# The order of every engine's instructions, taken from the scheduler's other machine model

## The chip, the cores and the metric

The kernel runs on one core of a Trainium2 chip. The time is the device time of one execution in microseconds. The profile names the engines PE (TensorE matmul), PEld (its weight loads), DVE (VectorE), ACT (ScalarE), POOL (GpSimd) and SP (SyncE, which here only issues DMAs).

## The reference, cut to what matters

One layer of a diffusion backbone over 1024 latent tokens with 1024 features and a context of 256 tokens, all in float32. Three sub-layers follow each other; each norms, modulates and gates its own result:

```python
h_lat = half_ffn(h_lat, ..., w13_a, w2_a)      # h + 0.5*gate*norm(swiglu(modulate(norm(h))))
h_ctx = half_ffn(h_ctx, ..., w13_a, w2_a)
h_lat, _ = token_mixing(h_lat, h_ctx, ...)     # one projection w_in of IN_WIDTH columns, then
#   a 2-D Fourier transform of 512 channels, and a bidirectional chunked mLSTM of 4 heads
#   (conv + silu on q and k, gates, chunks of 128 tokens, the context's final states first),
#   merged with sigmoid gates through w_four, w_mproj and w_out
h_lat = half_ffn(h_lat, ..., w13_b, w2_b)

def swiglu(u, w13, w2):
    a, b = jnp.split(u @ w13, 2, axis=-1)      # 1024 x 5632, then 2816 x 1024
    return (jax.nn.silu(a) * b) @ w2
```

## The kernel before, in words

Every large product is a sum of three matmuls on parts of the operands (`mm3`, L151 to L153): both operands are split into a high and a low part, and the product of the two low parts is left out. Tokens stand in two blocks of 512. A matmul is 128 x 128 against 128 x 512 and takes one bank of the accumulation memory.

Weights come in units of 1024 columns. `wload` issues the load on SP's queue (L124), `wunit` makes the high part on ACT (L138) and the low part on DVE (L139). The rings for the raw unit, the high part and the low part (`wr`, `wh`, `wl`) have three buffers each. Other tiles stand in rings with a fixed number of buffers too (`SLOTS`), and the accumulators in three: four banks `mm` for the large products, two `aux` and two `qc` for small ones.

The stages, in the order of time in the profile: setup and the first modulation; the first feed-forward half of the latents (`ffn_in`, a product of 2 x 2 blocks in seven multiplications, then `proj_out`); the same for the context; the token mixing (from about 930 to 2040 us), in which the projections of q, k, v and of the gates run among the small steps of the mLSTM and of the Fourier transform; the second feed-forward half, whose last product is token-major (`final`) and goes to the output.

The small steps are generators. `later` puts them in a list with a rate, and `tick`, called between the matmuls of a large product, advances them by that rate times the part of a weight unit done; `defer` calls a function a given number of units later. So the text of the program already has the small steps woven between the large products. Small matmuls that the prediction speaks of: L996 (transposing the gate rows, `gate_rows`), L1013 (the chunk's contribution to the state, `state_step`), L1039 and L1051 (the context's keys, `key_in` and `key_out`), L1198 (query times state), L1221 (`turn`), L1228 (`values`), L1239 (`store`), L1333 and L1341 (`fourier_rest`). Stores that it names: L474 (the gated product, `glu`) and L1112 (`gate_proj`).

The text is not the order in which the engines run. The tile framework records all instructions with their dependences. When the context closes, its scheduler plays the program through on a model of the machine. An engine of the model that is free takes, of its instructions whose operands and buffers are ready, the one written earliest. The order in which the model starts them becomes the fixed list of each engine and of each issuing queue, the buffers that tiles get are given out in the same play-through, and semaphores are put where one list needs another's result. On the chip each engine works its list from front to back. There are two such models in the framework: the default one and a second, the "timeline" model. They differ in what they charge for an instruction, a transfer and the way between engines.

Of the kernel before, what the change touches and what calls it, by code (L numbers as in the profile page):

```python
# [34 lines left out]
class Kernel:  # L35
# [15 lines left out]
    def defer(self, fn, parts=1.0):  # L51
        """fn is issued that many units of weights later, when its operands are sure to be there"""
        self.deferred.append([parts, fn])
# [92 lines left out]
    def mm3(self, out, st, mv, first, last):  # L146
        """out += st^T mv over the three products of the parts that carry weight in float32."""
        sh, sl = st
        mh, ml = mv
        mul = self.nc.tensor.matmul  # L150
        mul(out, sh, mh, start=first, stop=False)  # L151
        mul(out, sh, ml, start=False, stop=False)  # L152
        mul(out, sl, mh, start=False, stop=last)  # L153

# [66 lines left out]
    def ada_first(self):  # L221
        """shift and scale of the first half-step for both streams, the first half of the features"""
        nc = self.nc
        w = self.a["w_ada"][0]
        for ch in (1, 0):
# [5 lines left out]
            row = self.s512("t")  # L231
# [34 lines left out]
    def ada_cols(self, row, streams, ch, hf):  # L266
        """rows of the two streams -> columns, with the bias"""
# [9 lines left out]
    def pre(self, s, i, halves=(0, 1)):  # L277
        """per-feature scale g_pre*(1+scale) of sub-layer i (0..2) and the shift"""
# [12 lines left out]
    def post(self, s, i):  # L291
        """per-feature gate*g_post of sub-layer i, with the half of the half-steps"""
# [8 lines left out]
    def rstd_of(self, ssq, n, width, name=None):  # L301
        """(ssq/width + eps)^-0.5 on [128, n]"""
# [7 lines left out]
    def rows_bcast(self, rstd, n):  # L310
        """[128 tokens, n] -> PSUM [128, n*128], the value of each token in every partition"""
# [6 lines left out]
    def spread(self, rstd, T):  # L318
        """rstd in every partition"""
# [7 lines left out]
    def sumsq(self, tiles, T, out, name=None):  # L327
        """feature-major tiles [128, T] -> out[0]: rstd [128 tokens, T/128]"""
# [18 lines left out]
    def load_x(self, src, T, name, out, keep=False, tag="o"):  # L347
        """tokens from DRAM: the transpose to scratch, rstd of each token; out: scratch, rstd, tiles"""
# [44 lines left out]
    def prenorm(self, tiles, rstd, T, s, i, u, ds=range(ND)):  # L393
        """u = norm(h)*g*(1+scale) + shift, split; tiles: callable d -> [128, T]; rstd: list of one"""
# [26 lines left out]
    # The first product takes both blocks of 512 tokens at once, each pair of feature tiles as a product  # L421
    # of 2x2 blocks (token block x half of the inputs, half of the inputs x feature tile) in seven multiplications
    # after Winograd:
    #   s1 = a21+a22  s2 = s1-a11  s3 = a11-a21  s4 = a12-s2
    #   t3 = b22-b12  t2 = t3+b11  t1 = b12-b11  t4 = b21-t2
    #   p1 = a11 b11  p2 = a12 b21  p3 = s4 b22  p4 = a22 t4  p5 = s1 t1  p6 = s2 t2  p7 = s3 t3
    #   c11 = p1+p2  c12 = p1+p6+p5+p3  c21 = p1+p6+p7+p4  c22 = p1+p6+p7+p5
    NP = NF // 2

    def operands(self, tiles, rstd, u, s, i, out):  # L430
        """the sums over the normed tokens of both blocks, split; u: those of the first block"""
# [38 lines left out]
    def glu(self, p, g, gate, gs, j, b):  # L470
        """j: which feature tile of the pair, b: block of tokens"""
# [4 lines left out]
    def pair_weights(self, w, q, n0, W, p1s):  # L476
        """the combinations of weights of one pair of feature tiles (q even: those under silu, q odd: the others),
        in stages"""
# [50 lines left out]
    def pair_products(self, q, n0, W, U, gs, gates):  # L529
        """the products of one pair of feature tiles; yields the number of each"""  # L530
# [49 lines left out]
    def half_unit(self, w, p, k0):  # L580
        """half of the inputs of the first feature tiles of pair p"""
        return [w[:, k0 : k0 + 4, c : c + P] for c in (2 * p * P, FF + 2 * p * P)]

    def ffn_in(self, w13, n0, first, U, gs, early=0, mid=None):
        """silu(u w1)*(u w3) of both blocks to scratch; the products of the first block come first for n0 pairs.
        early: for so many pairs those of the first half of the inputs come before mid is called.
        Yields when room for operands of the next product comes free."""
# [77 lines left out]
    def g_loader(self, gs, b):  # L665
        """two feature tiles of the gated product, split"""
# [11 lines left out]
    def proj_out(self, w2, g, load=None, then=None, g2=None):  # L678
        """[K, 1024] weights on a feature-major operand: eight [128, 512] results.
        load: makes the operand during the first pass over it; then: the next operand, g2, during the last"""  # L680
# [29 lines left out]
    def residual(self, o, T, s, i, base, scr=None, c0=0, r=None, name=None):  # L710
        """in place: base + gate*norm(o); to scratch, with its rstd in r"""
        nc = self.nc
        q = []
# [96 lines left out]
    def ctx_residual(self, os, ssq, base, scr, r):  # L810
        """[two token tiles x two halves] -> h1 feature-major [128, 256] tiles to scratch"""
# [26 lines left out]
    def conv(self, xs, T, ct, out):  # L838
        """silu of the depthwise convolution over tokens (k scaled by 1/16); xs has a column to either side"""
# [10 lines left out]
    def tok_major(self, wcol, stat, ntt, sinks):  # L850
        """512 columns of w_in from wcol for ntt token tiles, token-major; sinks(tt, psum)"""
# [17 lines left out]
    def v_sink(self, v, nchunk, base, brow):  # L869
        """v: per head of the pair a list of tiles [128, 2, 257], two chunks each, a column of ones behind"""  # L870
# [27 lines left out]
    def gate_rows(self, psums, T, m0, full, nm, out):  # L898
        """rows 0-3: forward heads, rows 32-35: backward heads; T tokens per psum.
# [811 lines left out]
```

## Time and profile before

| | |
|---|---|
| median of 3 runs | 2786.73 us (2786.63 to 2790.77) |
| span of the profiled execution | 2784.4 us |
| PE busy | 2710.0 us (97%), 11937 matmuls |
| PEld busy | 2155.0 us (77%) |
| DVE busy | 1781.4 us (64%), 3147 instructions |
| ACT busy | 1071.4 us (38%), 1758 instructions |
| POOL busy | 97.7 us (4%), 214 instructions |
| granted TensorE clock, mean | 0.995 |
| DMA | 439.98 MB, mean 158 GB/s |

The span runs from the first to the last instruction of the profiled execution; the time of that execution is not listed beside it, and the median of the runs stands 2.3 us above the span. The matmuls are pipelined and the ends in their records are modelled, so an interval in which PE counts as busy may still hold less work than another. Idle time of an engine counts only where the engine sets the end.

### The profile page before, as it was taken

Reading aid. Unit: us, or ns where it says so; the run is one execution under the profiler, and the core shown is the slowest. Engines: PE = TensorE matmul, PEld = TensorE weight load, DVE = VectorE, ACT = ScalarE, POOL = GpSimd, SP = SyncE. Lnnn points to the kernel's source line nnn. Section 1 sums busy time; section 2 is a strip of 40 time slices with the busy share of each in tenths; the row PEclk is TensorE's granted clock in tenths of the full one; section 3 lists DMA queues with packets and bytes.
Section 4 is the critical chain, followed back from the end, with each engine's and each line's share of the span. In section 5 each row is a group of like instructions: output and inputs, shape, how many; then the busy total and the mean of one; then the engine's idle time right before and its main releaser. Section 6 shows DMA issues by size and latency. Waiting matters only on the chain.

```text
span 2784.4 us, 33892 instructions
## 1 busy us (share of the span) xinstructions
PE 2710.0 (97%) x11937; PEld 2155.0 (77%) x11937; DVE 1781.4 (64%) x3147; ACT 1071.4 (38%) x1758; POOL 97.7 (4%) x214
## 2 busy tenths in 40 slices
PE   8899999999999999999999999999999999999998
PEld 5688887778787777777777777778887788887777
DVE  6787777676585439465463765555759777763455
ACT  4543233343364336233332333334345323243443
POOL 1100000000000001000000000000002000000000
PEclk9999999999999999999999999999999999999999
DMA  8763434666486545324233442356547443335574
GB/s 302 242 204 110 137 110 147 205 227 203 142 259 204 171 133 173 90 79 143 71 97 104 140 135 58 108 163 208 190 149 233 136 136 114 118 106 164 196 249 166
DMA packets 414936, 439.98 MB, mean 158 GB/s; under 512 B 22105, under 2 KB 290946, under 8 KB 414768
## 3 DMA queue, kind: packets, MB, share of 16 engines
q1 hardware_dynamic: 413376, 436.01, 49.4%
q0 software_dynamic: 1248, 1.75, 0.3%
q8 instruction: 94, 1.54, 0.2%
q14 instruction: 74, 0.61, 0.1%
q10 hardware_dynamic: 144, 0.07, 0.0%
HBM read 360.10 MB, written 77.64 MB: 157 GB/s over the span
## 4 chain that ended last, share of the span: by engine, by line
PE 76%; DMA 9%; DVE 8%; issue 5%; ACT 2%; SPq 0%; POOL 0%; DVEq 0%; POOLq 0%; ACTq 0%
PE mm L153 22%; PE mm L151 22%; PE mm L152 22%; PE aux L1013 2%; DMA m<-r_l 2%; DVE wl L139 1%; PE qc L1198 1%; DMA ld<-in_w_ada_dram 1%; DMA wr<-gs 1%; DMA wr<-in_w_a_dram 1%; DMA wr<-in_w_b_dram 1%; DVE g L144 1%; DMA ld<-h 1%; ACT wh L138 1%; PE mm L230 1%
## 5 line engine op out<-in xcount | busy, mean ns | idle before, releaser
L139 DVE TENSOR_TENSOR wl<-wr,wh 128x1024 fp32r<-128x1024 f32 x342 | 414.1, 1211 | 376.6 <-ACT wh L138 375.6
L151 PE MATMUL mm<-g,wh 128*128 128x512 f32 (+1 forms) x1400 | 574.3, 410 | 5.5 <-ACT wh L138 5.5
L138 ACT CAST wh<-wr 128x1024 fp32r<-128x1024 f32 x342 | 352.9, 1032 | 558.5 <-PE mm L152 269.4
L153 PE MATMUL mm<-g,wl 128*128 128x512 f32 (+1 forms) x1400 | 558.8, 400 | 0.6 <-DVE wl L139 0.5
L152 PE MATMUL mm<-g,wh 128*128 128x512 f32 (+1 forms) x1400 | 558.4, 399 | 0.1
L151 PEld LDWEIGHTS mm<-g,wh 128*128 128x128 f32 (+1 forms) x1400 | 264.3, 189 | 67.1 <-ACT wh L138 6.6
L153 PEld LDWEIGHTS mm<-g,wl 128*128 128x128 f32 (+1 forms) x1400 | 263.7, 188 | 63.1 <-DVE wl L139 2.7
L152 PEld LDWEIGHTS mm<-g,wh 128*128 128x128 f32 (+1 forms) x1400 | 264.0, 189 | 58.7 <-issue 0.7
L151 PE MATMUL mm<-g,o 128*128 128x512 f32 x704 | 278.0, 395 | 0.0
L152 PE MATMUL mm<-g,o 128*128 128x512 f32 x704 | 277.9, 395 | 0.0
L153 PE MATMUL mm<-g,o 128*128 128x512 f32 x704 | 277.2, 394 | 0.0
L550 DVE TENSOR_TENSOR t<-mm,t 128x512 f32<-128x512 f32 x228 | 153.2, 688 | 85.5 <-PE mm L153 83.7
L151 PE MATMUL mm<-u,wh 128*128 128x512 f32 (+1 forms) x424 | 168.3, 399 | 8.1 <-DVE m L649 4.9
L153 PE MATMUL mm<-u,wl 128*128 128x512 f32 (+1 forms) x424 | 166.7, 396 | 3.1 <-DVE wl L139 3.1
L152 PE MATMUL mm<-u,wh 128*128 128x512 f32 (+1 forms) x424 | 167.7, 395 | 0.1
L153 PEld LDWEIGHTS mm<-g,o 128*128 128x128 f32 x704 | 132.3, 188 | 31.5
L151 PEld LDWEIGHTS mm<-g,o 128*128 128x128 f32 x704 | 132.2, 188 | 31.3
L152 PEld LDWEIGHTS mm<-g,o 128*128 128x128 f32 x704 | 132.2, 188 | 30.8
L151 PE MATMUL mm<-wh,g 128*128 128x512 f32 x280 | 112.2, 405 | 1.6 <-ACT b L1111 1.6
L152 PE MATMUL mm<-wl,g 128*128 128x512 f32 x280 | 111.4, 398 | 1.7 <-DVE wl L139 1.7
L153 PE MATMUL mm<-wh,g 128*128 128x512 f32 x280 | 111.1, 397 | 0.0
L151 PE MATMUL mm<-wh,u 128*128 128x512 f32 x272 | 108.9, 401 | 0.0
(545 smaller groups left out, 4199.7 us busy)
## 6 DMA issues: line engine op xcount, KB each, us to landing
wr<-in_w_a_dram SPq DMA_DIRECT2D x134, 512.0 KB, 4.1
wr<-in_w_b_dram SPq DMA_DIRECT2D x104, 512.0 KB, 3.9
wr<-in_w_in_dram SPq DMA_DIRECT2D x80, 512.0 KB, 3.5
gs<-m SPq DMA_DIRECT2D x88, 256.0 KB, 2.9
wr<-gs SPq DMA_DIRECT2D x44, 512.0 KB, 4.2
ld<-in_w_ada_dram SPq DMA_DIRECT2D x64, 256.0 KB, 2.8
ld<-h SPq DMA_DIRECT2D x56, 256.0 KB, 3.7
wr<-in_w_a_dram SPq DMA_DIRECT2D x40, 256.0 KB, 4.1
```

The costliest lines, as they stand in the source:

```text
L138: nc.scalar.copy(hv, rv)
L139: nc.vector.tensor_tensor(lv, rv, hv.bitcast(F32), op=ALU.subtract)
L144: self.nc.vector.tensor_tensor(lo, src, hi.bitcast(F32), op=ALU.subtract)
L151: mul(out, sh, mh, start=first, stop=False)
L152: mul(out, sh, ml, start=False, stop=False)
L153: mul(out, sl, mh, start=False, stop=last)
L230: nc.tensor.matmul(pt[:2, :], self.sc[:, k, :], t, start=k == 0, stop=k == ND - 1)
L550: add = lambda o, x, y: nc.vector.tensor_tensor(o, x, y, op=ALU.add)
L1013: nc.tensor.matmul(pt[:, :257], kw[:, i * P : (i + 1) * P], vaug, start=True, stop=True)
L1198: nc.tensor.matmul(pt[:, :257], at(q, i, c), C[:, i * 257 : (i + 1) * 257], start=i == 0, stop=i == 1)
```

## The change

One argument is added where the context is opened. It makes the scheduler play the program through on the timeline model in place of the default one. Instructions, tiles, rings and written order stay as they are. The other hunks of the diff delete comments and docstrings and leave the line numbers as they were; one of them stands here for all.

```diff
@@ -85,7 +85,7 @@
         self.bg.extend(gens)
         self.rate = rate
 
-    # ---- tiles ----
+
     def name(self, s):
         self.n += 1
         return f"{s}_{self.n}"
...
@@ -1704,7 +1704,7 @@
         arrays[f"in_{n}_dram"] = x
         a[n] = nc.dram_tensor(f"in_{n}_dram", x.shape, mybir.dt.from_np(x.dtype), kind="ExternalInput").ap()
     out = nc.dram_tensor("out_0_dram", (1, SEQ, D), F32, kind="ExternalOutput").ap()
-    with tile.TileContext(nc) as tc:
+    with tile.TileContext(nc, schedule_with_timeline_sim=True) as tc:
         emit(tc, a, out)
     r = _run(nc, [arrays], core_ids=[0])
     return r.results[0]["out_0_dram"]
```

## The prediction

> **What bounds the kernel now.** I read the page first (busy shares and clock), then the busy time by stretch, then PE's own waits in the stage that loses most, then a few microseconds of the timeline there.
>
> ```profile
> span 2784.4 us, 33892 instructions
> PE 2710.0 (97%) x11937; PEld 2155.0 (77%) x11937; DVE 1781.4 (64%) x3147; ACT 1071.4 (38%) x1758; POOL 97.7 (4%) x214
> PE 76%; DMA 9%; DVE 8%; issue 5%; ACT 2%; SPq 0%; POOL 0%; DVEq 0%; POOLq 0%; ACTq 0%
> ```
>
> PE is the bound: 97% busy, and 76% of the chain that ended last. Its work does not change here, so only the 74.4 us in which it idles (2784.4 - 2710.0) can be won, and any new idle time on it is lost in full. The same in stretches (the columns are start:end, length, then busy us and instruction count for PE, PEld, DVE, ACT, POOL, then the granted clock and the DMA share and GB/s):
>
> ```profile
> 0.00:130.00 130.00, 115.03 (x489) 81.64 (x489) 81.95 (x134) 66.78 (x126) 18.03 (x34) 0.99 0.85 282
> 130.00:470.00 340.00, 337.96 (x1452) 273.67 (x1453) 266.64 (x408) 114.26 (x188) 4.56 (x4) 0.99 0.45 136
> 1000.00:1900.00 900.00, 869.75 (x3907) 688.10 (x3906) 522.44 (x1349) 330.65 (x646) 39.85 (x144) 0.99 0.39 118
> 2170.00:2495.00 325.00, 325.00 (x1401) 262.76 (x1400) 240.86 (x372) 100.25 (x162) 0.00 (x0) 1.00 0.38 117
> 2495.00:2784.40 289.40, 271.69 (x1202) 217.17 (x1200) 139.03 (x166) 112.25 (x151) 4.43 (x5) 0.99 0.58 196
> ```
>
> The first row is the start, where data must first arrive: PE idles 15.0 us. The second and fourth are the two long products of the feed-forward halves: 2.0 us idle of 665, with DVE at 78% and 74%. The third is the token mixing: 30.2 us idle of 900. The last is the final product and the store: 17.7 us, part of it the end itself, where nothing is left for PE.
>
> **What the change moves.** No instruction is added or removed; the other hunks of the diff delete comments. What is rewritten is the order in which each of the five queues (PE, DVE, ACT, POOL, SP) holds its instructions, and with it which buffer of a ring a tile gets and so whose release it waits for. Each queue runs its list in order, so a wait on one instruction holds everything behind it (the row at 1047.72 below is one). The order comes from a play-through: an engine that is free takes the earliest written instruction that is ready by the model. Where the model is early about a result, the chip waits at that place; where it is late, ready work stands too far back. I cannot see from the trace what the second model charges, so I price the places at which the order decides.
>
> Term 1, the small matmuls in the token mixing. These (transposes, states, products of the recurrence) are written between the projections' matmuls and go into PE's list wherever the model thought their operands there. PE's waits from 1000 to 1900 us (us in all, times, longest):
>
> ```profile
> PE aux L1221 <- DVE m L1212: 6.2, 5, 2.4
> PE aux L1013 <- DVE m L1192: 6.2, 5, 2.6
> PE aux L1013 <- DVE st L1018: 4.5, 2, 3.2
> PE aux L1239 <- DVE m L1232: 4.0, 4, 1.7
> PE mm L1333 <- DMA ld<-z: 1.7, 1, 1.7
> PE mm L151 <- ACT b L1111: 1.6, 1, 1.6
> PE aux L1051 <- DVE ld L848: 1.4, 2, 1.1
> PE aux L1039 <- ACT u L1061: 1.2, 1, 1.2
> PE aux L996 <- ACT m L979: 1.1, 1, 1.1
> PE mm L1341 <- DVE acc L1339: 1.0, 1, 1.0
> PE aux L1013 <- DVE st L1016: 0.5, 2, 0.4
> PE aux L259 <- ACT rb L143: 0.2, 1, 0.2
> ```
>
> The nine "aux" rows are small matmuls: 25.3 us in 23 waits, 1.1 us each. That these are faults of placing and not lack of work shows in the timeline (start, us, then instruction; in brackets the idle time before it):
>
> ```profile
> 1046.11 0.39 PE L153 MATMUL mm<-wh,u 128*128 128x512 f32 x1
> 1047.72 0.33 PE L1039 MATMUL aux<-ident,u 128*128 128x128 f32 x1 [1.22 <-ACT u L1061]
> 1047.80 0.47 PE L151 MATMUL mm<-wh,u 128*128 128x512 f32 x1
> ```
>
> A projection's matmul ends its turn, PE waits 1.22 us for a transpose's operand, and 0.08 us after the transpose the next projection matmul starts without a wait of its own. An order with that transpose six matmuls later (0.23 us each, by 1401 in 325 us) loses nothing. So the term is bounded by -25.3 us if every such wait goes. On the other side stands the poorest 100 us of the same stage:
>
> ```profile
> 1200.00:1300.00 100.00, 92.61 (x410) 71.15 (x409) 61.59 (x190) 33.67 (x85) 2.87 (x8) 1.00 0.44 132
> 1300.00:1400.00 100.00, 98.85 (x446) 78.73 (x445) 46.42 (x116) 35.21 (x71) 3.54 (x10) 1.00 0.25 72
> ```
>
> At the first row's rate all 900 us would idle 9 x 7.39 = 66.5 us, 36.3 more than now; at the second's 9 x 1.15 = 10.4 us, 19.9 less. I take the second row as the nearest to what an order with better-placed small matmuls gives, since it holds the same mixture of recurrence and projections, and leave out of the gain the 4.3 us of the three "mm" rows (1.7 + 1.6 + 1.0), which wait for data of their own stage: -15.6 us.
>
> Term 2, weights. Each unit of weights is loaded from SP's queue, split on ACT and DVE, and used by some 24 matmuls.
>
> ```profile
> L139 DVE TENSOR_TENSOR wl<-wr,wh 128x1024 fp32r<-128x1024 f32 x342 | 414.1, 1211 | 376.6 <-ACT wh L138 375.6
> L138 ACT CAST wh<-wr 128x1024 fp32r<-128x1024 f32 x342 | 352.9, 1032 | 558.5 <-PE mm L152 269.4
> wr<-in_w_a_dram SPq DMA_DIRECT2D x134, 512.0 KB, 4.1
> PE mm L151 <- ACT wh L138: 6.0, 4, 2.5
> PE mm L153 <- DVE wl L139: 4.3, 6, 2.1
> PE mm L152 <- DVE wl L139: 2.2, 3, 1.7
> SPq L124 <- DVE wl L139: 619.0, 259, 11.9
> ```
>
> A unit takes 4.1 + 1.03 + 1.21 = 6.3 us from issue to use. Three buffers hold 3 x 24 x 0.23 = 16.6 us of PE's work, so with two units ahead (11.0 us) some 4.7 us of queueing on SP, ACT and DVE is covered. SP spends 619 us waiting for a free buffer at its loads, so it normally asks as early as it can; what stands behind such a wait on SP (a store, or another load) is held with it. The covering fails now 13 times for 12.5 us over the whole run. A new order can win at most these 12.5 us. It can lose too: a store on SP whose data comes late, or other DVE work placed before a split, uses up the 4.7 us. The price nearest to this is a hundred microseconds of the second half's product in which DVE is fuller:
>
> ```profile
> 2100.00:2200.00 100.00, 97.30 (x425) 78.39 (x426) 83.30 (x118) 46.76 (x74) 14.41 (x7) 1.00 0.61 190
> 2200.00:2300.00 100.00, 100.00 (x432) 80.84 (x431) 77.07 (x120) 28.20 (x46) 0.00 (x0) 1.00 0.42 127
> ```
>
> 2.7 us in 100 would be 18.0 us over the 665 us of the two long products, 16.0 beyond the 2.0 lost there now. Between -12.5 and +16.0 I take 0: the rows of these products show PE full under an order that a model of the same kind made.
>
> Term 3, start, end and POOL: 0. The first loads and the last stores have no other work to change places with. POOL is busy 97.7 us in all, DVE and ACT have 36% and 62% to spare, and what moves on them is hidden behind PE unless it reaches Terms 1 or 2.
>
> Sum: -15.6 us. The profiled span of 2784.4 becomes 2768.8. The median of the three runs shown, 2786.73, stands 2.3 us above that span, so I forecast 2771 us (-0.6%). A change within 0.2% (5.6 us) is about what cannot be told from none.
>
> The Trainium skill ("Perfetto Trace Analysis", Identifying the Most-Contended Engine) says matmul busy time is a poor measure of the distance from the limit and that the weight loads' busy share is a better one. The trace agrees that more than PE's idle time is lost: PEld is 80.85% in the full stretch from 2170 to 2495 us and 76.5% in the token mixing.
>
> **The rivals.**
>
> Slower by the same place (31%): the other model is earlier than the chip about DVE's and ACT's results in the recurrence, and the small matmuls wait more than now. Each wait costs 1.1 us (25.3 in 23), so five waits more decide for slower, and there are many chances for one; the line of the states alone has
>
> ```profile
> L1013 PE MATMUL aux<-u,kw 128*128 128x257 f32 x224 | 63.3, 394 | 10.6 <-DVE m L1192 6.2 <-DVE st L1018 4.5
> ```
>
> Half of the way to the poorest window is +18 us, 2805 us; the whole way +36.3, 2823. For it: that the present order waits only 23 times there, and the rates at which work is written between the units (`later`, `credit`, `defer`) stand as constants beside the present order. Against: it waits at all where work was ready.
>
> No measurable change (17%), 2787: PE's list is mostly fixed by the written order and by data. In the two long products nothing can be gained, and in the token mixing some waits go and others come. The case that the option changes no order at all is in here; nothing in the profile speaks for it.
>
> A larger gain (6%): the token mixing reaches the pace of the full stretch by PEld. 0.8085 x 900 = 727.7 us of weight loads fit, 688.1 are there: 39.6 / 0.8085 = 49 us, so 2738. Against it: its many narrower matmuls cannot keep that share.
>
> Long waits (6%): weights and small matmuls are both late, and waits grow from about 1 us to several. These are dearer than their length, because PE's clock falls:
>
> ```profile
> 1700.00:1800.00 100.00, 96.43 (x428) 75.94 (x427) 57.13 (x153) 38.90 (x80) 3.54 (x10) 0.97 0.28 83
> ```
>
> A mean clock of 0.97 is 6 us of these 100 at half speed, 3 us lost. With 36.3 us of Term 1 and 16.0 of Term 2 the time is 2839, and each such fall of the clock comes on top of that. The Trainium skill ("TensorE: Matmul & The Clock Gate", Part 1: The HAM clock gate) puts the fall to half speed after an idle window of about 3.4 us. The waits quoted above are mostly below that and the clock is 1.00 in most rows, which agrees.
>
> **How the numbers follow.** Forecast 40%, larger gain 6%, no change 17%, slower by waits 31%, long waits 6%. Faster by over 0.2%: 46%; within: 17%; slower: 37%. The likeliest case's own range is 2749 (25.3 of Term 1 and 12.5 of Term 2 won in full) to 2781 (the edge of no change). The whole range goes from 2749 to the full price of the slower rival, 2823; outside are the larger gain (6%), the long waits (6%) and some 6% of the slower rival that add part of Term 2.
>
> **What would show it.** Right: in the trace of the changed kernel PE idles 14 to 16 us from 1000 to 1900 us, the "aux" waits sum to about 10 us, and the waits for L138 and L139 stay near 12.5. Wrong in Term 1: "aux" waits above 25 us, or the same sum at other lines. Wrong in Term 2: PE below 100% in the two long products, with L138 or L139 as what it waits for, or SP waiting longer at a store (L474, L1112) with a load of weights behind it. If PE's idle time is as before but the span is not, the loss is inside its busy time, in narrower spacing or in the clock. The forecast is also wrong if the order at the start puts loads of x behind others: the first 130 us are outside the sum.

## The result: 0.9% slower

The changed kernel takes 2812.18 us (median of 4 runs, 2812.10 to 2813.68), the kernel before in the same session 2787.03 us: a ratio of 1.009, interval 1.0076 to 1.0105, 25 us more. Below, "the new order" is that of the changed kernel and "the old order" that of the one before. First the head of the page of the profile after:

```profile
span 2811.8 us, 33833 instructions
PE 2723.8 (97%) x11937; PEld 2169.8 (77%) x11937; DVE 1772.1 (63%) x3147; ACT 1067.0 (38%) x1758; POOL 94.2 (3%) x214
PE 81%; DMA 8%; DVE 6%; ACT 2%; issue 2%; SPq 0%; DVEq 0%; POOL 0%; POOLq 0%; ACTq 0%
```

The same 11937 matmuls are there. The span is 27.4 us longer, half of it in PE's idle time (88.0 us, before 74.4) and half in its busy time (13.8 us more); the mean granted clock fell from 0.995 to 0.988, so the same matmuls took longer. Some of the stretches that answer to those shown of before (columns as there: length, busy us and counts of PE, PEld, DVE, ACT, POOL, then the granted clock, DMA share, GB/s):

```profile
1000.00:1900.00 900.00, 861.72 (x3818) 682.28 (x3817) 506.54 (x1333) 327.03 (x640) 39.49 (x144) 0.98 0.39 113
1300.00:1400.00 100.00, 100.00 (x459) 82.27 (x458) 52.20 (x149) 36.05 (x75) 5.01 (x16) 1.00 0.26 70
1400.00:1500.00 100.00, 90.12 (x400) 69.65 (x399) 48.33 (x165) 32.56 (x76) 3.87 (x7) 0.97 0.32 90
1800.00:1900.00 100.00, 84.24 (x339) 64.54 (x338) 54.43 (x159) 33.59 (x75) 4.19 (x7) 0.90 0.41 119
2170.00:2495.00 325.00, 315.08 (x1348) 254.60 (x1347) 250.27 (x383) 104.12 (x168) 4.27 (x3) 0.98 0.40 122
```

From 1000 to 1900 us seven of the nine hundreds are better than before: 1200 to 1300 idles 4.2 us instead of 7.4, 1300 to 1400 nothing instead of 1.2, 1700 to 1800 1.0 instead of 3.6. Two are worse. From 1400 to 1500 us PE idles 9.9 us instead of 4.3, and by far the worst is the end of the last head: from 1800 to 1900 us PE idles 15.8 us at a clock of 0.90. The same stretch of before:

```profile
1800.00:1900.00 100.00, 97.37 (x434) 78.81 (x433) 55.75 (x121) 33.36 (x62) 2.17 (x4) 1.00 0.51 160
```

That is 13.1 us more idle, and a mean clock of 0.90 is 20 us of the 100 at half speed (the last section shows stretches at 0.50), some 10 us lost: about 23 us together. Counting PE's large matmuls (L151 to L153, 10320 in each kernel) gives the same figure by another way: number 6600, early in the merge, starts at 1899.0 us after and 1875.7 us before, 23.3 us apart, and up to 1800 us PE had idled about as long in both (47.0 us after, 50.4 before). But number 6450 started 22.4 us *earlier* than before. The new order had run ahead with its large products. It fell back by 45 us over the next 150: some 25 us of that is idle time and clock, and the rest is small matmuls that it had left for later.

The second place is at 2200 us: the full stretch from 2170 to 2495 us, which idled nothing before, idles 9.9 us, in one wait (us in all, times, longest):

```profile
PE mm L151 <- ACT o L143: 9.9, 1, 9.9
```

```profile
2190.00:2196.10 6.10, 6.10 (x27) 4.65 (x25) 4.34 (x7) 0.59 (x1) 0.78 (x1) 1.00 0.62 200
2196.10:2200.50 4.40, 0.04 (x1) 0.00 (x0) 4.01 (x7) 1.35 (x2) 0.00 (x0) 1.00 0.47 128
2200.50:2206.10 5.60, 0.04 (x1) 0.04 (x1) 5.57 (x11) 2.99 (x6) 0.00 (x0) 0.50 0.60 175
2206.10:2210.80 4.70, 4.70 (x11) 3.73 (x12) 3.87 (x7) 2.09 (x4) 0.00 (x0) 0.51 0.25 75
```

PE stands before the first of the seven multiplications of the second half until an operand is cast (`o` in L143, a combination of weights). The clock halves 4.4 us into the wait, and the matmuls of the next 4.7 us run at a clock of 0.51. By the count of large matmuls this costs 11 us (from +19.9 at number 7800 to +30.9 at 7950). The rest of the run gives some 7 us back (the merge and the last stretch idle 3.3 and 2.8 us less).

Why was PE ahead with large products and then without work? One step of one chunk in head 3 shows it. L1212 on DVE makes the products that L1221 on PE turns (start, us, instruction). Before:

```profile
1789.20 0.35 DVE L1212 SCALAR_TENSOR_TENSOR m<-m,den,m 128x128 f32<-128x128 f32 x1
1789.60 0.33 PE L1221 MATMUL aux<-ident,m 128*128 128x128 f32 x1
```

After, the same step of another chunk of head 3, with the first and the last of the matmuls in between:

```profile
1808.99 0.35 DVE L1212 SCALAR_TENSOR_TENSOR m<-m,den,m 128x128 f32<-128x128 f32 x1
1809.55 0.39 PE L153 MATMUL mm<-g,wl 128*128 128x512 f32 x1
...
1815.05 0.39 PE L152 MATMUL mm<-g,wh 128*128 128x512 f32 x1
1815.28 0.27 PE L1221 MATMUL aux<-ident,m 128*128 128x128 f32 x1
```

Before, the turn starts 0.05 us behind its operand. After, it starts 5.94 us behind it, with 21 large matmuls and four state matmuls (L1013) in front. Over all 32 chunks (mean time from the operand's end to PE's start; the last column is the mean distance from one chunk's L1232 to the next's):

| | L1212 to L1221 | L1222 to L1228 | L1232 to L1239 | a chunk |
|---|---|---|---|---|
| before | 0.98 us | 1.50 us | 4.79 us | 11.44 us |
| after | 4.19 us | 2.81 us | 6.93 us | 13.62 us |

Little of this is a wait of PE, and so the table of PE's waits doesn't show it; it shows in who waits for whom (us in all, times). The first row of each fence is the idle time of PE and its weight loads ahead of L1221, until DVE's L1212 was done; the second is what DVE's L1229 waited for PE's L1228. Before:

```profile
  DVE m L1212: 15.1, 12
  DVE m L1229: 28.6, 15
```

After:

```profile
  DVE m L1212: 0.2, 1
  DVE m L1229: 78.6, 24
```

In the old order PE stands until the small step is ready. In the new one PE is kept full and DVE waits. The last chunk of the last head then ends late, and the large products that ran beside it end early. The last chunk's last matmul (L1239, last start), what ACT takes from the last gate product (L1111, last start) and the merge's last sum (L1406, last start), before and then after:

```profile
L1239 PE MATMUL aux<-ident,m x64: 271/272/421, 1261.8 to 1839.9; 128*128 128x128 f32 x64
L1111 ACT ACTIVATE b<-mm,cc x48: 662/686/694, 950.4 to 1842.9; 128x512 f32<-128x512 f32 x48
L1406 DVE SCALAR_TENSOR_TENSOR t<-t,mm x16: 677/679/689, 1846.2 to 2017.1; 128x512 f32<-128x512 f32 x16
```

```profile
L1239 PE MATMUL aux<-ident,m x64: 270/272/421, 1280.7 to 1876.6; 128*128 128x128 f32 x64
L1111 ACT ACTIVATE b<-mm,cc x48: 662/684/699, 952.6 to 1820.6; 128x512 f32<-128x512 f32 x48
L1406 DVE SCALAR_TENSOR_TENSOR t<-t,mm x16: 679/681/689, 1825.1 to 2040.3; 128x512 f32<-128x512 f32 x16
```

The last chunk is 36.7 us late, and the gate products end 22.3 us early. Before, they outlast the last chunk by 3.0 us; after, they end 56.0 us ahead of it. In these 56 us PE has the rest of head 3 and the first products of the merge, and the operands of the merge come in piece by piece. By the source (`merge_in`) the first block of the merge needs 512 tokens, so of head 3 only the first four chunks. But its loads (L1376) stand in SP's list between the stores of the last chunks (L1245):

```profile
1855.78 0.36 SPq L1245 DMA_DIRECT2D hn<-m  x1
...
1862.62 0.36 SPq L1245 DMA_DIRECT2D hn<-m  x1
1864.33 1.35 SPq L1376 DMA_DIRECT2D ld<-hn  x2
```

By the written order these two loads take rows of heads 1 and 2, which end at 1527.5 and 1743.3 us. Whether their place in SP's list or a buffer held them is not shown.

The merge's end is 23.2 us late. Behind the last chunk nothing more is lost: from there to the merge's end PE's list has 681 large matmuls after and 756 before, which take 163.7 and 177.2 us, and PE idles 2.0 and 0.1 us of it.

### The profile page after: what moved, and what is told of

It reads as the page before. It is cut to its first block, busy times and chain, and to the rows that moved or that the text cites. A ratio compares the mean times of both kernels' runs of the same rounds, so it can differ in the third digit from the quotient of the medians.

```text
span 2811.8 us, 33833 instructions
## 1 busy us (share of the span) xinstructions
PE 2723.8 (97%) x11937; PEld 2169.8 (77%) x11937; DVE 1772.1 (63%) x3147; ACT 1067.0 (38%) x1758; POOL 94.2 (3%) x214
## 4 chain that ended last, share of the span: by engine, by line
PE 81%; DMA 8%; DVE 6%; ACT 2%; issue 2%; SPq 0%; DVEq 0%; POOL 0%; POOLq 0%; ACTq 0%
PE mm L151 23%; PE mm L152 23%; PE mm L153 23%; PE aux L1013 2%; PE qc L1198 2%; DMA ld<-h 1%; DVE wl L139 1%; DMA wr<-in_w_b_dram 1%; DVE g L144 1%; DMA wr<-gs 1%; ACT wh L138 1%; DMA g<-in_w_ada_dram 1%; DMA wa<-in_w_ada_dram 1%; DMA ld<-hn 1%; DMA wr<-in_w_a_dram 1%
## 5 line engine op out<-in xcount | busy, mean ns | idle before, releaser
L139 DVE TENSOR_TENSOR wl<-wr,wh 128x1024 fp32r<-128x1024 f32 x342 | 412.8, 1209 | 356.8 <-ACT wh L138 351.4
L151 PE MATMUL mm<-g,wh 128*128 128x512 f32 (+1 forms) x1400 | 564.0, 403 | 5.7 <-ACT wh L138 3.7
L153 PE MATMUL mm<-g,wl 128*128 128x512 f32 (+1 forms) x1400 | 558.6, 400 | 1.8 <-DVE wl L139 1.5
L138 ACT CAST wh<-wr 128x1024 fp32r<-128x1024 f32 x342 | 352.4, 1032 | 509.6 <-PE mm L152 251.0
L151 PEld LDWEIGHTS mm<-g,wh 128*128 128x128 f32 (+1 forms) x1400 | 263.7, 188 | 68.4 <-ACT wh L138 4.4
L153 PEld LDWEIGHTS mm<-g,wl 128*128 128x128 f32 (+1 forms) x1400 | 263.2, 188 | 64.0 <-DVE wl L139 3.5
L151 PE MATMUL mm<-g,o 128*128 128x512 f32 x704 | 278.6, 396 | 9.9 <-ACT o L143 9.9
L153 PE MATMUL mm<-g,o 128*128 128x512 f32 x704 | 277.7, 395 | 0.0
L151 PE MATMUL mm<-u,wh 128*128 128x512 f32 (+1 forms) x424 | 168.6, 406 | 15.1 <-DVE wa L620 5.7
L153 PE MATMUL mm<-u,wl 128*128 128x512 f32 (+1 forms) x424 | 167.2, 397 | 0.0
L151 PEld LDWEIGHTS mm<-g,o 128*128 128x128 f32 x704 | 132.8, 189 | 41.6 <-ACT o L143 10.3
L153 PEld LDWEIGHTS mm<-g,o 128*128 128x128 f32 x704 | 132.6, 188 | 31.3
L153 PE MATMUL mm<-wh,g 128*128 128x512 f32 x280 | 111.7, 400 | 0.0
L151 PEld LDWEIGHTS mm<-u,wh 128*128 128x128 f32 (+1 forms) x424 | 81.0, 192 | 37.7 <-ACT u L143 6.0
L152 PE MATMUL mm<-wl,u 128*128 128x512 f32 x272 | 108.4, 398 | 1.8 <-DVE wl L139 1.7
```

Of the source, the lines that this page charges most:

```text
L138: nc.scalar.copy(hv, rv)
L139: nc.vector.tensor_tensor(lv, rv, hv.bitcast(F32), op=ALU.subtract)
```

## The experiments

Each ratio is to the kernel before in the same session, whose median lay between 2787 and 2794 us. The changed kernel itself stands at 1.009; the same order measured again, in another session, stands at 1.0072 (1.0054 to 1.0090; see "The second place"). A ratio between 1.005 and 1.009 is therefore not told from no change. Any edit makes the scheduler play the program through anew, so an edit of the changed kernel can move more than it names.

### Put the large products of the gates back behind the small steps

Theory of the time: the large products run ahead, and a tie that holds them back restores the old time. The edit marks the first matmul of every four k-steps of a projection so that it stays behind all that was written before it on PE.

```
-        mul(out, sh, mh, start=first, stop=False)
+        (self.tc.keep_in_program_order if pin else id)(mul(out, sh, mh, start=first, stop=False))
```

In the last head only:

> The changed kernel, with one thing undone in the last head alone: each group of four contraction steps of a q, k or gate product may not enter PE's list before the small matmuls written ahead of it. Theory (cover): the timeline model's order puts large products ahead of the mLSTM's small steps, so that at the end of the last head nothing is left to run beside them. Then the 23 us lost between 1800 and 1900 us go: about 2789 us, PE idle in that window below 5 us instead of 15.8, clock back to 1.00. Rival (waits of small matmuls, as in the prediction's Term 1): the loss is many short waits over all four heads, and this wins 3 us at most. Rival (buffers): the loss comes from which buffer a tile gets and when it comes free; then 2812 stays.

In all heads:

> The changed kernel with the same tie in all four heads. Cover: the ends of the first three heads (windows 1400 to 1500 and 1600 to 1700 us, PE 90 and 95 busy of 100) fill up too, 2780 to 2790 us. Waits of small matmuls: tying more large products behind small ones makes PE wait more, slower than with the last head alone. Buffers: 2812.

And the tie of the last head on the kernel before, as a control:

> Control: the kernel before (default model) with the tie in the last head. Cover: its order has the small steps in place already, so within 0.2% of 2787 us. If the tie itself were worth 20 us whatever the model, this would come to about 2767.

Measured: 1.012 (1.0105 to 1.0135) in the last head, 1.0373 (1.0357 to 1.0388) in all heads, 1.0064 (1.0048 to 1.0081) on the kernel before. The tie alone costs some 18 us in the old order, so it could not undo anything. It is too rigid: with it PE waits 5.1 us at L1239 and 4.9 us at L1221 for DVE in single waits, which the changed kernel didn't have, and in the last head the last chunk ends 14.3 us later still. Holding large products strictly behind small steps costs more than either order.

### More cover for the last head

The 21 gate products are dealt to the heads 4, 4, 5, 8 instead of 6, 5, 5, 5.

```
-            for _ in range((len(todo) + HEADS - 1 - h) // (HEADS - h)):
+            for _ in range((4, 4, 5, 8)[h]):
```

> The changed kernel with the 21 remaining gate products dealt 4, 4, 5, 8 to the four heads in place of 6, 5, 5, 5: the last head has three more, 3 x 48 matmuls x 0.23 us = 33 us of cover. Cover: about 15 to 20 us of the 23 come back (2792 to 2797), the earlier heads having the next head's products to run beside them. Buffers: 2812, since the same tiles turn over in the same rings. Waits of small matmuls: within 5 us of 2812.

Measured: 1.0063 (1.0047 to 1.0078), at most some 7 us won where 15 to 20 were expected, and not told from the 1.0072 of the repeated order. Heads 1, 2 and 3 begin 20 to 28 us earlier, but with eight products beside it head 3 takes 120 us from its first chunk to its last instead of 101, and the last chunk comes only 1.8 us earlier than in after. PE's idle time moved: from the last gate product to the merge's end it is 6.4 us instead of 15.8, and from 950 us to that product 29.9 instead of 22.5. Cover that is added to one head is taken from the others, and it is also work that stands in front of the head's small steps.

### Lengthen the chain in the old order

The second kernel has 8 in place of 4.

```
             nc.scalar.copy(B[:, P : 2 * P], pt[:, :P])
+            [nc.scalar.copy(*x) for x in ((A[:, 256:384], B[:, P : 2 * P]), (B[:, P : 2 * P], A[:, 256:384])) * 4]
```

> The kernel before, in its own order, with eight extra 128x128 copies on ACT inside each chunk of a head, between the copy of the turned products (L1222, 0.3 us) and the values' matmul (L1228). Nothing else is changed; ACT gets about 256 x 0.3 = 77 us more work in a stretch where it is busy 327 of 900 us. The chain of one chunk becomes about 2.6 us longer, which is the size of the difference between the two kernels' paces (11.44 us and 13.62 us a chunk). Theory A (the time was lost because the chain of each head is slower, so that the large products run ahead and the end of the last head stands uncovered): pace 13 to 14.5 us, time 15 to 30 us above before (ratio 1.005 to 1.011). Theory B (the chain's pace is covered, and the loss comes from the order of the large products, their weights and their buffers): within 0.3% of before (0.997 to 1.003).

> The same with sixteen copies, about 5.2 us a chunk. Theory A: the loss grows about in proportion, 35 to 60 us above before (1.012 to 1.022), pace 16 to 17 us. Theory B: within 0.5% of before, since ACT still has room.

Measured: 1.0082 (1.0055 to 1.0110) and 1.0143 (1.0122 to 1.0164). Both times fall into the range of theory A, but not by its mechanism. PE's waits in the two, from 1000 to 1900 us:

```profile
PE aux L1228 <- ACT m L1222: 21.0, 13, 3.0
```

```profile
PE aux L1228 <- ACT m L1222: 35.2, 20, 4.5
```

The old order lets PE stand before L1228 thirteen and twenty times. Other waits became shorter, so PE's idle time in this window grows by less than these 21.0 and 35.2 us: to 44.0 and 51.4 us, from 30.2 in before. That is 13.8 and 21.2 us, a good half of the loss (23 and 40 us). A chunk took 12.03 us in the first and 14.11 in the second, where 13 to 14.5 and 16 to 17 were expected. So this doesn't test whether a slow chain costs cover. It shows the other way of losing: a delay that the order doesn't hide is paid at the wait.

### Fewer turns of one ring of PSUM banks

In the heads, six small results of a chunk take turns in the two banks of `aux`. With late small matmuls each turn is slow. Two of the six are moved to `qc`, which also has two banks.

```
         def turn(c):
-            pt = self.aux()
+            pt = self.aux("qc")
         def store(c):
-            pt = self.aux()
+            pt = self.aux("qc")
```

> The kernel after, with the PSUM tiles of the turned products and of a chunk's output taken from the ring of qc instead of the ring of aux; each has two banks. The ring of aux then turns four times a chunk instead of six, and a chunk's first product has to wait for fewer small matmuls of the chunk before it. Theory A: the pace of a chunk falls from 13.6 us by 1 to 4 us and the time by 5 to 20 us against after (ratio to before 1.002 to 1.007). If the rings don't set the pace, or the ring of qc takes their place: the time of after (1.009), pace unchanged. Theory B: the time of after within 0.2%, even where the pace falls.

Measured: 1.0014 (1.0002 to 1.0026), against 1.009 of the changed kernel without it: most of the loss is gone, more than Theory A asked for. L1212 to L1221 falls to 2.91 us and L1232 to L1239 to 5.25 us. The pace falls by only 0.4 us, to 13.18, where Theory A asked for 1 to 4; head 3 takes 95 us instead of 101. The last chunk and the merge's end:

```profile
L1239 PE MATMUL qc<-ident,m x64: 270/272/421, 1279.2 to 1865.5; 128*128 128x128 f32 x64
L1406 DVE SCALAR_TENSOR_TENSOR t<-t,mm x16: 679/682/690, 1821.3 to 2029.4; 128x512 f32<-128x512 f32 x16
```

11.1 us earlier the one, 10.9 us the other. The profiled execution (2800.17 us) was the longest of the ten, 5.5 us above their median, so the trace shows less of the gain than the ratio. The wait at the second place is still there (10.8 us). From 1257.8 us on PE's list is another one than in the changed kernel, so how much of the gain is due to the fewer turns, and how much to the new list, is not shown.

### The second place: issue the operands earlier

```
         for p in range(early, n0):
-            if p == n0 - 1:
+            if p == n0 - 2:
                 self.drain()
```

> The kernel after, with one line changed in the second feed-forward: the rest of the operands of the second half's Winograd products is issued in full one pair of feature tiles earlier (at the last pair but one). In after PE waits 9.9 us for the first of these products at about 2196 us and runs at half clock for some us behind it, and the curve of its large products loses 11 us there against before. Theory: the wait shrinks below 3 us and the time falls by 6 to 12 us (ratio to before 1.005 to 1.007). Rival: the operands' work is held up by ACT, DVE and the ring of PSUM, not by when it is issued; then the wait stays within 2 us of 9.9 and the time is that of after.

Measured: 1.0072 (1.0054 to 1.0090). The wait is still there:

```profile
PE mm L151 <- ACT o L143: 10.4, 1, 10.4
```

But the edit changed nothing. In its trace the list of every engine, from PE's 11937 matmuls to the loads on SP, holds the same instructions in the same order as that of the changed kernel. So neither the theory nor its rival is tested, and the run is a repeat of the changed kernel: the last chunk comes at 1873.7 us instead of 1876.6, and the ratio is 1.0072 instead of 1.009.

What the two traces show of the place is this. The cast that PE waits for takes a sum of DVE's (L509), which itself takes one of L508. Before, the one follows the other at once:

```profile
2164.38 0.69 DVE L508 TENSOR_TENSOR wa<-wr 128x512 f32<-128x512 f32 x1 [5.78 <-DMA wr<-in_w_b_dram]
2165.10 0.69 DVE L509 TENSOR_TENSOR wa<-wa,wr 128x512 f32<-128x512 f32 x1
```

After, 12.1 us lie between them, in which DVE works on the sums over tokens:

```profile
2191.86 0.68 DVE L508 TENSOR_TENSOR wa<-wr 128x512 f32<-128x512 f32 x1
2204.67 0.68 DVE L509 TENSOR_TENSOR wa<-wa,wr 128x512 f32<-128x512 f32 x1
```

In after the cast is done when 7848 large matmuls have started, which is when PE runs out; in before at 7807. The sums over tokens are late as well. On their way the small matmuls that add up squares (L343, to the copy that ACT makes of what comes of them) take 7.8 and 8.5 us in after, 3.5 and 3.6 us in before, so a part is the same lateness. Whether L509 was held by its place in DVE's list or by a buffer is not shown.

### Does it begin before head 0?

In after head 0's first chunk is already 28.0 us late (1248.1 against 1220.1 us). Before it stand the context's states, 91 us long instead of 26 us from the first update to the last store, because each of their small products lies some 5 us back on PE; the gates and the first transposes of head 0 follow them in the rings `st` and `aux`. Three edits free them from it: the gates' running maximum in another tile, the states' products in `qc`, and the states' products in turn in both rings.

```
-        ... for tag in ("uuuuu" if hb else ("m", "m", "m", "m", "st"))
+        ... for tag in ("uuuuu" if hb else ("m", "m", "m", "m", "acc" if full else "st"))
...
...
-            pt = self.aux()
+            pt = self.aux(tags[i])
```

In the second edit `tags` is `("qc", "qc")` or `("aux", "qc")` for the context's states, and two times `"aux"` elsewhere. The running maximum alone, on the changed kernel, with the change of the ring above, and on the kernel before alone and with the ring:

> The kernel after, with one buffer changed: the running maximum of the gates' first half (cleared at L923) is kept in the tile acc instead of in the ring st, whose four tiles the context's states use up to 1201 us (1110 us in before). In after that clearing stands at 1184.5 us (1106.2 us in before) and the first chunk of head 0 begins 27.9 us later than in before (1248.1 against 1220.1 us); the last chunk of head 3 ends 36.8 us later. Theory C (the serial chain from the context's states over the gates to the last chunk of head 3 is what the kernel now ends on, and most of its delay arises before head 0 begins): head 0 begins at 1218 to 1232 us, the last chunk ends 15 to 28 us earlier than in after, and the time falls by as much: ratio to before 0.999 to 1.004. Rival D (only the pace inside the heads counts, and what is won before head 0 is lost again because the keys and queries aren't there earlier): ratio 1.007 to 1.010.

> The kernel after with both changes: the running maximum in acc, and the turned products and the chunk's output in the ring of qc. Theory C: the two gains add, since one is before head 0 and the other inside the heads: 25 to 40 us below after, ratio to before 0.994 to 1.000. Rival D: no better than the ring alone (1.001).

> Control: the kernel before with the running maximum in acc. There the clearing waits for nothing long (1106.2 us, right behind the transfers ahead of it). Theory C: within 0.3% of before, since head 0 does not begin earlier. If it gained 0.5% or more, the change of buffer would be a gain of its own and a_acc would not tell of the scheduler.

> Control: the kernel before with both changes. In before the last chunk of head 3 ends 35.6 us ahead of the first products that need it, 15 us more than the least distance seen in the other runs (20 to 22 us), so a faster chain should buy little: within 0.4% of before (0.996 to 1.004). If the rings held the chain in before too, it gains 5 to 15 us (0.995 to 0.998).

The states in `qc` as well, the control for it, the states in both rings, and all of it with the change of the ring in the heads:

> The kernel after, with the small products of the context's states in the PSUM ring qc (free at that time) instead of aux, and the running maximum of the gates in acc instead of st. Nothing of the gates or of head 0's keys then stands behind the states in a ring. Theory C' (the context's states, 91 us long in after because each of their small products stands some 5 us late in PE's list, hold the aux ring, and with it the gates' columns, the first transposes of the keys and the whole chain of the heads): the columns come before 1180 us (1212.6 in after), head 0's first transposes at 1175 to 1195 us (1212.5), its first chunk at 1210 to 1230 us (1248.1), the last chunk of head 3 ends 15 to 35 us earlier than in after, ratio to before 0.997 to 1.004. Rival D' (head 0 begins earlier, but the later heads wait for their own keys, values or buffers, so that little arrives at the end): last chunk less than 8 us earlier, ratio 1.006 to 1.010. Rival E (the keys themselves come late): head 0's first transposes stay at 1205 us or later.

> Control: the kernel before with the same two changes of ring. There the states take 26 us and are done at 1110 us, 57 us before the gates' last columns. Theory C': within 0.3% of before.

> The kernel after, with the two small products of each of the context's states one in aux and one in qc: four banks instead of two for the same chain. Theory C': the states take 45 to 65 us instead of 85 (from 1110 us on), the gates' clearing comes at 1140 to 1160 us, the columns at 1170 to 1190, head 0's first chunk 15 to 30 us earlier than in after, ratio to before 0.998 to 1.005. If each state waits for the one before it and not for a bank, the states stay at 80 us or more and nothing is gained (1.008 to 1.010).

> The kernel after with all of it: the states in qc, the running maximum in acc, and in the heads the turned products and the chunk's output in qc. Theory C': the gains before head 0 and inside the heads add: 25 to 45 us below after, ratio to before 0.992 to 1.000. Rival D': that of the ring alone, 1.000 to 1.003.

| kernel | ratio, interval | head 0 begins | head 1 begins | last chunk | against after |
|---|---|---|---|---|---|
| after | 1.0090 (1.0076 to 1.0105) | 1248.1 | 1422.7 | 1876.6 | |
| after, `acc` | 1.0101 (1.0080 to 1.0123) | 1253.3 | 1432.1 | 1887.5 | +10.9 |
| after, `acc` and the ring | 1.0051 (1.0034 to 1.0068) | 1255.3 | 1432.8 | 1877.4 | +0.8 |
| after, states in `qc`, and `acc` | 1.0105 (1.0084 to 1.0127) | 1235.8 | 1425.8 | 1883.8 | +7.2 |
| after, states in both rings | 1.0058 (1.0043 to 1.0073) | 1231.2 | 1420.3 | 1873.7 | -2.9 |
| after, states in `qc`, `acc` and the ring | 1.0023 (1.0013 to 1.0033) | 1233.1 | 1420.2 | 1863.9 | -12.7 |
| before, `acc` | 1.0004 (0.9992 to 1.0016) | | | | |
| before, `acc` and the ring | 0.9997 (0.9984 to 1.0010) | | | | |
| before, states in `qc`, and `acc` | 0.9999 (0.9988 to 1.0009) | | | | |

(Times in us within each kernel's profiled execution; the last chunk is the last start of L1239.) The last three columns come from one execution of each kernel and are rough. The kernel before with the states in `qc` and `acc` has its last chunk at 1851.5 us, 11.6 us later than before, at a ratio of 0.9999. The same order as in after had its own 2.9 us earlier. So a shift of less than some 12 us between sessions is not told from none.

By their ratios Theories C and C' fall: 1.0101 and 1.0105, where 0.999 to 1.004 and 0.997 to 1.004 were asked for. Without the states ahead of them, head 0's first transposes came at 1190.4 us, as expected of C', and its first chunk 12.3 us earlier, at 1235.8 us, where C' asked for 1210 to 1230. But head 1 began no earlier than in after, and neither did the last chunk come earlier: what is won ahead of head 0 is lost again before head 1, as D' said. With the states in both rings head 0 began 16.9 us earlier, and the last chunk only 2.9 us. The ring in the heads lowers the ratio each time: from 1.009 to 1.0014 on after, from 1.0101 to 1.0051 with `acc`, from 1.0105 to 1.0023 with the states in `qc` as well, and in the last two pairs, measured within one session each, the last chunk comes 10.1 and 19.9 us earlier. On the kernel before the three edits that were tried, the ring among them, do nothing that can be measured. There PE's list stayed nearly the same, and the small matmuls were not late.

In all these kernels what follows the last chunk is the same. With the states in `qc`:

```profile
L1239 PE MATMUL aux<-ident,m x64: 270/273/422, 1261.7 to 1883.8; 128*128 128x128 f32 x64
L1406 DVE SCALAR_TENSOR_TENSOR t<-t,mm x16: 675/680/689, 1833.7 to 2047.9; 128x512 f32<-128x512 f32 x16
```

A distance of 164.1 us again. In the ten kernels in the new order that have no tie it lies between 162.0 and 164.3 us, while the last chunk moves by 24 us (1863.9 to 1887.5). This does not show that the merge waits for the last chunk: the same 681 large matmuls stand between the two in PE's list in all ten, and PE is nearly full there. It shows that the loss lies ahead of the last chunk.

### The backward pass of the last head

In before, the first chunk of each head takes its last queries (L1189, the second half of its product) 0.1 to 0.7 us behind their convolution (L848): it waits for them. In after it takes them 26 to 34 us behind it, with the backward pass over the states in between. That pass is left out for head 3 in both kernels, so part of the computation is missing. Two of the four changed lines:

```
-            Cb[c - 1] = self.slot("o")
-            self.state_step(kw.pop(c), va(c), db[:, 4 + h, c : c + 1], Cb[c], Cb[c - 1])
+            Cb[c - 1] = self.slot("o") if h < 3 else Cb[c]
+            if h < 3: self.state_step(kw.pop(c), va(c), db[:, 4 + h, c : c + 1], Cb[c], Cb[c - 1])
```

> The kernel after without the backward pass over the states in head 3: its 14 small products and their updates are left out, and every chunk of that head uses the loaded backward state (so part of the computation is missing). The work left out is some 6 us of PE. Theory F (the merge waits for the last chunk of head 3, and that head is late in after because its backward pass stands between the queries and the first chunk: 35 us behind the last query's convolution): the first chunk of head 3 comes 12 to 30 us earlier than in after (1775.4 us), the last chunk and the merge as much, time 12 to 28 us below after, ratio to before 0.999 to 1.005. Rival G (the end of the last head is set by its own pace and by the large products alone): no more than the 6 us of work, ratio 1.006 to 1.009.

> The kernel before without the backward pass in head 3, as a control for the work that is left out. There head 3's first chunk waits for the queries (1746.3 us against the convolution at 1748), not for the pass. Theory F: its first chunk moves by no more than the work left out, 2 to 8 us, and so does the time: ratio 0.997 to 1.000. Rival G: the same. If it gains 12 us or more, the pass was on the path in before too.

Measured: 1.0054 (1.0039 to 1.0069) from 1.009, and 0.9968 (0.9955 to 0.9981) from 1. The changed kernel gains some 5 to 10 us (from the 1.0072 of the repeat or from 1.009) and the kernel before 9. Theory F asked for head 3's first chunk 12 to 30 us earlier and for a gain in the first well beyond that in the second. The first chunk came at 1774.9 us instead of 1775.4, so F falls; rival G fits, with a price of the pass nearer 9 us than 6. In the changed kernel the transposes of the keys remain and still take 16 us, and the first chunk still takes its last queries 25 us behind the convolution. The backward pass by itself isn't what makes the new order slower.

## Why the prediction was wrong

The forecast was 2771 us; the time is 2812. The sign is wrong; the range, 2749 to 2823, holds the time.

**The step that failed** is in Term 1: "An order with that transpose six matmuls later (0.23 us each, by 1401 in 325 us) loses nothing." The new order did just this, with 21 matmuls instead of six. For PE at that place it is true. For the chain that the small matmul belongs to it isn't: each step put back is added to a chain of three or four such steps a chunk and 32 chunks, and a chunk took 13.62 us instead of 11.44. Large matmuls put in front are also gone later on: the gate products ended 56.0 us ahead of the last chunk, where before they outlasted it by 3.0, and there PE idled 15.8 us of 100 at a clock of 0.90. The prediction priced the small matmuls by PE's own waits and left the lateness of their results, and the use of the large ones, at zero.

**The size of Term 1.** The waits that were to shrink to some 10 us are these (1000 to 1900 us, after):

```profile
PE qc L1198 <- ACT m L1214: 11.8, 7, 1.9
PE aux L1013 <- DVE m L1229: 5.2, 2, 2.7
PE qc L1198 <- DVE st L1018: 3.0, 1, 3.0
PE aux L1013 <- ACT g L1157: 1.2, 2, 0.6
PE aux L996 <- ACT m L979: 1.0, 1, 1.0
PE aux L1228 <- ACT m L1222: 0.8, 1, 0.8
...
PE aux L1156 <- DVE o L1018: 0.6, 2, 0.4
PE aux L1189 <- DVE m L1229: 0.5, 1, 0.5
PE aux L1156 <- ACT g L1157: 0.5, 1, 0.5
...
PE aux L1013 <- DVE m L1192: 0.3, 1, 0.3
PE aux L271 <- ACT b L262: 0.2, 1, 0.2
```

They sum to 25.1 us in 20, against 25.3 us in 23 before: "the same sum at other lines", which the prediction named as the sign that Term 1 is wrong. The old waits at L1221 and L1239 are gone, as forecast, and others came at L1198. The window that served as the nearest, 1300 to 1400, did become better, to no idle time at all. It was no measure of the stage, because an order that fills one window takes the large products from a later one. The stage as a whole idles 38.3 us instead of 30.2, and its last hundred loses some 10 us more to the clock.

**Term 2** was set to 0. The waits for L138 and L139 didn't turn into a loss (11.8 us over the run, before 12.5). But the second of the long products, in which PE was full before, lost 9.9 us to a single wait. Its operand is a combination of weights that L143 casts, a path that Term 2 did not have. **Term 3**, 0: the start idles 2.0 us more, the end 2.8 us less.

**The rivals.** "Slower by the same place" came out, within its prices (2805 to 2823), though not for its reason: it expected more waits of the small matmuls because the model is early about DVE and ACT. Here small matmuls are placed late. "Long waits" was right about the clock: it is 0.50 from 4.4 us into the wait of 9.9 us, and the end of the last head runs at 0.90. The Trainium skill ("TensorE: Matmul & The Clock Gate", Part 1: The HAM clock gate), by which an idle window of about 3.4 us halves the clock, agrees with the row of 0.50; the last section has the other.

**What is shown and what is open.** Shown: the two places and their size; that small matmuls stand further behind their operands; that the gate products end early and the last chunk late, and that PE idles between the two; and that moving two results to another ring recovers most of the loss (1.009 to 1.0014, and a half to four fifths of it beside other edits). Argued only is that the late small matmuls are the cause of the late last chunk: no run changed that alone. Not shown is how the 36.7 us by which the last chunk is late are made up in full. The context's states, head 0's start and the backward pass have been taken out, and none is the cause by itself. Nor is it shown what the second model charges that makes it place the small matmuls so, or what holds DVE's L509 back at the second place. No version that computes the whole is measurably faster than the kernel before.

## What to carry to other kernels

When an order is to be rewritten, price a small instruction by how far it stands behind its operand and how long the chain is that it belongs to, and not by the waits of the engine that it sits on: an engine kept full can still be losing time, and it shows as other engines waiting for it. Compare the end of such a chain with the end of the large products that run beside it: what an order spends early in filling waits is missing at the end. If results of such a chain share a ring of two banks, try them in two rings. Before an edit is believed to test something, see in its trace that the lists of the engines changed.

## What the runs showed of the hardware that was not expected

In the wait of 9.9 us the clock fell to 0.50 after 4.4 us and stayed there for 4.7 us of matmuls behind it. In the last head no single wait reaches 3.5 us, yet the clock falls as well:

```profile
1840.00:1880.00 40.00, 29.51 (x108) 21.36 (x106) 22.26 (x80) 12.96 (x36) 2.16 (x4) 0.83 0.36 100
1828.50:1831.90 3.40, 3.40 (x8) 2.74 (x9) 0.97 (x3) 0.48 (x1) 0.00 (x0) 0.50 0.42 115
1845.50:1848.90 3.40, 3.40 (x12) 2.75 (x11) 0.58 (x2) 1.39 (x5) 0.00 (x0) 0.50 0.22 69
1869.40:1876.20 6.80, 5.68 (x15) 3.87 (x14) 3.67 (x9) 2.20 (x7) 0.54 (x1) 0.50 0.57 172
```

PE's longest waits from 1800 to 1900 us are 3.4 us, right ahead of the stretch at 1828.50, and 3.0 us, 1.3 us ahead of the one at 1845.50. The waits after these are below 2 us, and the clock is at 0.50 again from 1869.40 on. In the 40 us of the first row PE is busy 74% of the time, partly with small matmuls. So shorter waits brought the clock down too, at least where many small matmuls stand between them; which of the two it takes is not shown. It cost some 10 us on top of the 13.1 us of added idle time. The Trainium skill ("TensorE: Matmul & The Clock Gate", A second HAM failure mode: psum-queue depth-cycling) describes a kernel in which frequent short idles between groups of matmuls make the clock swing between half and full; these rows agree with it.
